# RMS norm with ReLU on one core: hardware loops with explicit semaphores, stores moved to Pool's software queue

## The chip, the cores and the metric

The kernel runs on one core of one Trainium2 chip; the other cores are idle. The metric is the device time of one execution in microseconds (us), as a median of several runs. The profiled execution has a "span", which is about 2 us shorter than the device time. All runs quoted here were with a granted clock of 1.0.

The engines matter as follows. ScalarE (ACT in the profile) squares and sums the rows. VectorE (DVE) scales them. SyncE (SP) only issues transfers and waits. Pool (GpSimd) does almost nothing in the kernel before (four fills, 0.2 us). Sixteen DMA engines move all data between HBM and the on-chip memory (SBUF): the page counts 33.56 MB read from HBM and 33.55 MB written.

## The reference

```python
x = randn(16, 1024, 512)            # float32; gamma = ones(512), eps = 1e-5
rms = np.sqrt(np.mean(x ** 2, axis=-1, keepdims=True) + eps)
out = np.maximum(x / rms * gamma, 0)
```

The input has 33.55 MB and the output as many. Each byte is read once and written once, so at least 67.11 MB must move.

## The kernel before

The 16,384 rows are cut into 8 chunks of 128 partitions x 16 rows x 512 numbers, 4.19 MB each. A chunk is loaded by one transfer, computed in place in two groups of 8 rows per partition, and stored by one transfer. There are six chunk buffers ("slots"), so the last two loads wait for the first two stores.

```python
def load(i):  nc.sync.dma_start(out=slot[i % nslots], in_=xv[i])
def store(i): nc.sync.dma_start(out=ov[i], in_=slot[i % nslots])

def compute(i):
    xt = slot[i % nslots]
    for g in range(ngroups):                       # 2 groups of 8 rows
        a, b = g * G, (g + 1) * G
        for j in range(a, b):
            nc.scalar.activation(out=junk, in_=xt[:, j, :], func=ACTF.Square,
                                 accum_out=ss[i][:, j:j + 1])
        nc.scalar.activation(out=rms[i][:, a:b], in_=ss[i][:, a:b],
                             func=ACTF.Sqrt, bias=eps_sb, scale=inv_d)
        nc.vector.tensor_mul(out=xt[:, a:b, :], in0=xt[:, a:b, :], in1=gammaG())
        nc.vector.reciprocal(out=rstd[i][:, a:b], in_=rms[i][:, a:b])
        for j in range(a, b):
            nc.vector.tensor_scalar(out=xt[:, j, :], in0=xt[:, j, :],
                scalar1=rstd[i][:, j:j + 1], scalar2=0.0,
                op0=ALU.mult, op1=ALU.max)
# ... (gamma is broadcast to all partitions; 6 loads are issued, 6 chunks computed)
nxt = nslots
for i in range(nchunks):
    store(i)
    if i >= 1 and nxt < nchunks:
        load(nxt); compute(nxt); nxt += 1
```

Everything is unrolled, and a framework places the waits. All loads and stores stand in one line on SyncE's hardware queue.

## Time and profile before

| | |
|---|---|
| time, median | 164.2 us (164.16 to 164.38, 3 runs) |
| span | 162.0 us |
| bytes moved | 67.11 MB |
| one 32 KB packet on one engine | 1.213 us, 27.0 GB/s |
| the engines' shortest total | 2,048 packets / 16 x 1.213 us = 155.3 us |
| first packet starts, last one ends | 1.75 us, 160.64 us |

First come lines of the profile's page: the span; the busy time of the engines; the busy share of VectorE and of the DMA engines in 40 equal slices (tenths); the queue with its packets, MB and share of the 16 engines' time; and the chain of waits by engine.

```profile
span 162.0 us, 554 instructions
...
DVE 124.6 (77%) x164; ACT 98.5 (61%) x274; POOL 0.2 (0%) x4
...
DVE  1001299999999999999999999999999999920000
...
DMA  6999899999999999998999999999999999999990
...
q1 hardware_dynamic: 2304, 67.11, 96.9%
...
DVE 74%; DMA 8%; ACT 3%; issue 2%; DVEq 0%
```

The DMA engines are busy from end to end (96.9%); VectorE is busy for 77% and has nothing to do in the last four slices. The chain of waits names VectorE first, with 74%. That chain follows only semaphores; it doesn't know that the last stores stand in line behind others. So the row of slices, not the chain, tells the bound here.

The rate is 433 GB/s, except for a dip to 385 where the first loads end and the stores begin (56 to 64 us).

Now VectorE. These are the groups of instructions of the page: count, total busy us and mean ns of one, then idle time before them.

```profile
L78 DVE TENSOR_TENSOR slot<-slot,gamma_sb 128x4096 f32<-128x4096 f32 x16 | 70.7, 4418 | 4.2 <-ACT junk L74 4.2
L81 DVE TENSOR_SCALAR slot<-slot,rstd 128x512 f32<-128x512 f32 x128 | 52.1, 481 | 0.6
```

And this is one group of 8 rows in time order (start us, length us, engine, line, operation), followed by the end of VectorE's work and the last store.

```profile
26.83 4.42 DVE L78 TENSOR_TENSOR slot<-slot,gamma_sb 128x4096 f32<-128x4096 f32 x1
31.17 0.19 DVE L79 RECIPROCAL rstd<-rms 128x8 f32<-128x8 f32 x1
31.40 3.26 DVE L81 TENSOR_SCALAR slot<-slot,rstd 128x512 f32<-128x512 f32 x8
34.57 4.42 DVE L78 TENSOR_TENSOR slot<-slot,gamma_sb 128x4096 f32<-128x4096 f32 x1
```

```profile
141.32 1.67 DVE L81 TENSOR_SCALAR slot<-slot,rstd 128x512 f32<-128x512 f32 x4
143.01 0.33 SPq L62 DMA_DIRECT2D out_dram<-slot  x1
```

One group takes 34.57 - 26.83 = 7.74 us: a product over 8 rows (4.33 to the next start), a reciprocal (0.23) and eight scalings (0.396 each). The last store is issued at 143.01 us, 19 us before the end. So VectorE has about 5 us to spare. This is an estimate: the first 15 of 16 chunk transfers take 15/16 x 155.3 = 146 us from 1.75 us on, and with the dip the engines would run dry near 149 us; the last store must be ready about 1 us before that.

### The profile page before, as it was taken

The numbers are of one execution on the slowest core, as the hardware profiler recorded it, in microseconds if no ns is written. First come the engines' busy times: TensorE is split into PE (matmuls) and PEld (weight loads), VectorE is DVE, ScalarE is ACT, GpSimd is POOL, SyncE is SP. The second block draws the span as 40 slices with busy tenths as digits, with TensorE's granted clock in tenths as the row PEclk, the third lists the DMA queues.
The fourth block names the chain that finished last, engine by engine and source line by source line (L and its number), as shares of the span: only waits on it lengthen the run. The fifth ranks groups of instructions, "written<-read, shape, count | busy, mean of one in ns | idle before, by whom it ended". The sixth has DMA issues, their size and how long they took to land.

```text
span 162.0 us, 554 instructions
## 1 busy us (share of the span) xinstructions
DVE 124.6 (77%) x164; ACT 98.5 (61%) x274; POOL 0.2 (0%) x4
## 2 busy tenths in 40 slices
DVE  1001299999999999999999999999999999920000
ACT  2107999999999999999999199901998000000000
POOL 0000000000000000000000000000000000000000
DMA  6999899999999999998999999999999999999990
GB/s 227 421 405 502 388 413 493 390 421 477 396 421 471 396 388 388 461 445 388 463 437 404 453 445 404 453 437 396 461 429 445 429 421 445 429 421 445 437 413 16
DMA packets 2315, 67.14 MB, mean 414 GB/s; under 512 B 260, under 2 KB 260, under 8 KB 264
## 3 DMA queue, kind: packets, MB, share of 16 engines
q1 hardware_dynamic: 2304, 67.11, 96.9%
q14 instruction: 3, 0.02, 0.0%
q10 hardware_dynamic: 8, 0.01, 0.0%
HBM read 33.56 MB, written 33.55 MB: 414 GB/s over the span
## 4 chain that ended last, share of the span: by engine, by line
DVE 74%; DMA 8%; ACT 3%; issue 2%; DVEq 0%
DVE slot L78 43%; DVE slot L81 30%; DMA slot<-in_x_dram 8%; ACT junk L74 3%; DVE rstd L79 1%; DVEq L133 0%
## 5 line engine op out<-in xcount | busy, mean ns | idle before, releaser
L74 ACT ACTIVATE junk<-slot 128x512 f32<-128x512 f32 x128 | 76.8, 600 | 23.0 <-DMA slot<-in_x_dram 19.5
L78 DVE TENSOR_TENSOR slot<-slot,gamma_sb 128x4096 f32<-128x4096 f32 x16 | 70.7, 4418 | 4.2 <-ACT junk L74 4.2
L81 DVE TENSOR_SCALAR slot<-slot,rstd 128x512 f32<-128x512 f32 x128 | 52.1, 481 | 0.6
L74 ACT ACTIVATION_READ_ACCUMULATOR junk<-slot 128x1 f32 x128 | 23.8, 186 | 0.0
L93 DVE LOAD_MASK_SELECT gamma_sb<-gseed x1 | 0.0, 14 | 12.8 <-DMA gseed<-in_gamma_dram 12.8
L76 ACT ACTIVATE rms<-ss,eps_sb 128x8 f32<-128x8 f32 x16 | 4.8, 301 | 0.5
L74 ACT ACT_TABLE_LOAD x1 | 1.3, 1283 | 3.2 <-issue 3.2
L79 DVE RECIPROCAL rstd<-rms 128x8 f32<-128x8 f32 x16 | 3.1, 194 | 0.0
L76 ACT ACT_TABLE_LOAD x1 | 1.3, 1283 | 0.0
L86 DVE MEMSET gseed<- 128x512 f32 x1 | 0.5, 485 | 0.9 <-PEq L119 0.9
L93 DVE STREAM_SHUFFLE gamma_sb<-gseed 128x512 f32<-128x512 f32 x1 | 0.7, 721 | 0.0
L119 POOL MEMSET const-bfloat16-1.0<- 128x1 bf16 x1 | 0.1, 101 | 0.0
L119 POOL MEMSET const-uint8-127<- 128x1 uint8 x1 | 0.1, 101 | 0.0
L119 POOL MEMSET const-float32-0.0<- 128x1 f32 x1 | 0.1, 99 | 0.2 <-issue 0.2
L119 POOL MEMSET const-float32-1.0<- 128x1 f32 x1 | 0.1, 98 | 0.0
L87 DVE MEMSET eps_sb<- 128x1 f32 x1 | 0.1, 59 | 0.0
## 6 DMA issues: line engine op xcount, KB each, us to landing
slot<-in_x_dram SPq DMA_DIRECT2D x8, 4096.0 KB, 30.6
out_dram<-slot SPq DMA_DIRECT2D x8, 4096.0 KB, 35.4
gseed<-in_gamma_dram ACTq DMA_DIRECT2D x4, 2.0 KB
```

The source lines that it names most:

```text
L74: nc.scalar.activation(out=junk, in_=xt[:, j, :], func=ACTF.Square, accum_out=ss[i][:, j:j + 1])
L76: nc.scalar.activation(out=rms[i][:, a:b], in_=ss[i][:, a:b], func=ACTF.Sqrt, bias=eps_sb, scale=inv_d)
L78: nc.vector.tensor_mul(out=xt[:, a:b, :], in0=xt[:, a:b, :], in1=gammaG())
L79: nc.vector.reciprocal(out=rstd[i][:, a:b], in_=rms[i][:, a:b])
L81: nc.vector.tensor_scalar(out=xt[:, j, :], in0=xt[:, j, :], scalar1=rstd[i][:, j:j + 1], scalar2=0.0, op0=ALU.mult, op1=ALU.max)
L86: nc.vector.memset(gseed, 0.0)
L87: nc.vector.memset(eps_sb, eps)
L93: nc.vector.stream_shuffle(gamma_sb, gseed, [0] * 32)
L119: nc = _bacc.Bacc("TRN2", target_bir_lowering=False, num_devices=1)
```

## The change

The change moves the stores from SyncE's queue to Pool's software queue (`software_dynamic` in the profile; Pool is busy for at least 0.53 us with each issue), and holds the first store until the fourth load has landed. ScalarE and VectorE each run a hardware loop of 16 turns with addresses taken from registers, and all waits become explicit semaphores. TensorE merely passes on "chunk has landed". VectorE's arithmetic is regrouped: the multiplications by the row's factor and by gamma become one fused instruction per row, and the max becomes one large instruction per group. The square root's table is loaded ahead of time (the trace of before has two table loads of 1.28 us). ScalarE's scratch output gets room for eight rows instead of one; its squares then come 0.61 us apart instead of 0.75.

```diff
-    def store(i): nc.sync.dma_start(out=ov[i], in_=slot[i % nslots])
+    def store(i): nc.gpsimd.dma_start(out=ov[i], in_=slot_ap(i)).then_inc(sem_st[i], 16)
+    # SyncE
+    for i in range(nchunks):
+        if i >= nslots:
+            nc.sync.wait_ge(sem_st[i - nslots], 16)
+        load(i)
+    # Pool
+    nc.gpsimd.wait_ge(sem_ld[3], 16)                 # the fourth load
+    for i in range(nchunks):
+        nc.gpsimd.wait_ge(done, per * (i + 1))       # per = 2 groups in a chunk
+        store(i)
     # ScalarE: ... the same squares and square roots, in Fori(0, 16), Sqrt table preloaded
-            nc.vector.tensor_mul(out=xt[:, a:b, :], in0=xt[:, a:b, :], in1=gammaG())
-            nc.vector.reciprocal(out=rstd[i][:, a:b], in_=rms[i][:, a:b])
-            for j in range(a, b):
-                nc.vector.tensor_scalar(out=xt[:, j, :], in0=xt[:, j, :],
-                    scalar1=rstd[i][:, j:j + 1], scalar2=0.0, op0=ALU.mult, op1=ALU.max)
+        with nc.vector.Fori(0, ngroups) as gi:
+            nc.vector.wait_ge(sq, 1); nc.vector.sem_inc(sq, -1)
+            base = nc.vector.snap((gi % (nslots * per)) * (G * d))
+            col = nc.vector.snap(gi * G)
+            nc.vector.reciprocal(out=rstd[:, bass.ds(col, G)],
+                                 in_=rms[:, bass.ds(col, G)]).then_inc(sv, 1)
+            nc.vector.wait_ge(sv, 1); nc.vector.sem_inc(sv, -1)
+            for j in range(G):
+                row = slots[:, bass.ds(base + j * d, d)]
+                r = nc.vector.scalar_tensor_tensor(out=row, in0=row,
+                    scalar=rstd[:, bass.ds(col + j, 1)], in1=gamma_sb,
+                    op0=ALU.mult, op1=ALU.mult)
+                if j == G - 1: r.then_inc(sv, 1)
+            nc.vector.wait_ge(sv, 1); nc.vector.sem_inc(sv, -1)
+            nc.vector.tensor_scalar_max(out=blk, in0=blk, scalar1=0.0).then_inc(done, 1)
```

More of the change, by code (lines that the diff above doesn't have):

```diff
@@ L31 @@
     inv_d = 1.0 / d
-    xv = x2.rearrange("(c p k) d -> c p k d", p=P, k=16)
-    ov = out2.rearrange("(c p k) d -> c p k d", p=P, k=16)
     K = 16
@@ L38 @@
     nslots = 6
-    ngroups = K // G
+    ngroups = rows // G
+    per = K // G
+    xv = x2.rearrange("(c p k) d -> c p k d", p=P, k=K)
+    ov = out2.rearrange("(c p k) d -> c p k d", p=P, k=K)
     singles = ctx.enter_context(tc.tile_pool(name="singles", bufs=1))
-    slots = ctx.enter_context(tc.tile_pool(name="slots", bufs=1))
-    small = ctx.enter_context(tc.tile_pool(name="small", bufs=1))
     psum = ctx.enter_context(
         tc.tile_pool(name="psum", bufs=1, space=bass.MemoryType.PSUM))
-    ctx.enter_context(tc.manual_schedule())
     gseed = singles.tile([P, d], F32, name="gseed")
@@ L51 @@
     eps_sb = singles.tile([P, 1], F32, name="eps_sb")
-    junk = psum.tile([P, d], F32, name="junk")
-    slot = [slots.tile([P, K, d], F32, name=f"slot{s}") for s in range(nslots)]
-    ss = [small.tile([P, K], F32, name=f"ss{i}") for i in range(nchunks)]
-    rms = [small.tile([P, K], F32, name=f"rms{i}") for i in range(nchunks)]
-    rstd = [small.tile([P, K], F32, name=f"rstd{i}") for i in range(nchunks)]
+    ss = singles.tile([P, rows], F32, name="ss")
+    rms = singles.tile([P, rows], F32, name="rms")
@@ new lines @@
+    rstd = singles.tile([P, rows], F32, name="rstd")
+    slots = singles.tile([P, nslots * K * d], F32, name="slots")
+    junk = psum.tile([P, G, d], F32, name="junk")
+    sem_ld = [tc.alloc_semaphore(f"ld{i}") for i in range(nchunks)]
+    sem_st = [tc.alloc_semaphore(f"st{i}") for i in range(nchunks)]
+    sem_g = tc.alloc_semaphore("gam")
+    sem_e = tc.alloc_semaphore("epsr")
+    sem_z = tc.alloc_semaphore("zero")
+    ready = tc.alloc_semaphore("ready")
+    sq = tc.alloc_semaphore("sq")
@@ L58, in load, with slot_ap @@
+    done = tc.alloc_semaphore("done")
+    sa = tc.alloc_semaphore("sa")
+    sv = tc.alloc_semaphore("sv")
+    def slot_ap(i):
+        s = (i % nslots) * K * d
+        return slots[:, s:s + K * d].rearrange("p (k d) -> p k d", d=d)
     def load(i):
-        nc.sync.dma_start(out=slot[i % nslots], in_=xv[i])
+        nc.sync.dma_start(out=slot_ap(i), in_=xv[i]).then_inc(sem_ld[i], 16)
     def store(i):
-        nc.sync.dma_start(out=ov[i], in_=slot[i % nslots])
-    def gammaG():
-        g = gamma_sb[:]
-        return bass.AP(tensor=g.tensor, offset=g.offset,
-                       ap=[g.ap[0], [0, G], g.ap[1]])
@@ L69, in compute @@
-    def compute(i):
-        xt = slot[i % nslots]
-        for g in range(ngroups):
-            a, b = g * G, (g + 1) * G
-            for j in range(a, b):
-                nc.scalar.activation(out=junk, in_=xt[:, j, :], func=ACTF.Square,
-                                     accum_out=ss[i][:, j:j + 1])
-            nc.scalar.activation(out=rms[i][:, a:b], in_=ss[i][:, a:b],
-                                 func=ACTF.Sqrt, bias=eps_sb, scale=inv_d)
-            nc.vector.tensor_mul(out=xt[:, a:b, :], in0=xt[:, a:b, :], in1=gammaG())
-            nc.vector.reciprocal(out=rstd[i][:, a:b], in_=rms[i][:, a:b])
-            for j in range(a, b):
-                nc.vector.tensor_scalar(
-                    out=xt[:, j, :], in0=xt[:, j, :],
-                    scalar1=rstd[i][:, j:j + 1], scalar2=0.0,
-                    op0=ALU.mult, op1=ALU.max)
@@ L86 @@
-    nc.vector.memset(gseed, 0.0)
-    nc.vector.memset(eps_sb, eps)
-    for q in range(0, P, 32):
-        nc.scalar.dma_start(out=gseed[q:q + 1, :], in_=gamma[None, :])
-    for i in range(min(nslots, nchunks)):
-        load(i)
-    nc.vector.stream_shuffle(gamma_sb, gseed, [0] * 32)
-    for i in range(min(nslots, nchunks)):
-        compute(i)
-    nxt = nslots
-    for i in range(nchunks):
-        store(i)
-        if i >= 1 and nxt < nchunks:
-            load(nxt)
-            compute(nxt)
-            nxt += 1
+        nc.gpsimd.dma_start(out=ov[i], in_=slot_ap(i)).then_inc(sem_st[i], 16)
@@ new lines @@
+    ctx.enter_context(tc.manual_schedule(engines={mybir.EngineType.SP}))
+    with tc.tile_critical():
+        for i in range(nchunks):
[3 more added lines that the diff above has]
+        for i in range(nchunks):
+            nc.tensor.wait_ge(sem_ld[i], 16)
+            nc.tensor.sem_inc(ready, per)
+        nc.gpsimd.wait_ge(sem_ld[min(3, nchunks - 1)], 16)
+        for i in range(nchunks):
+            nc.gpsimd.wait_ge(done, per * (i + 1))
+            store(i)
+        nc.vector.memset(gseed, 0.0).then_inc(sem_z, 1)
+        nc.vector.memset(eps_sb, eps).then_inc(sem_e, 1)
+        nc.scalar.wait_ge(sem_z, 1)
+        for q in range(0, P, 32):
+            nc.scalar.dma_start(out=gseed[q:q + 1, :],
+                                in_=gamma[None, :]).then_inc(sem_g, 16)
+        nc.scalar.preload_act_table(ACTF.Sqrt)
+        nc.scalar.wait_ge(sem_e, 1)
+        with nc.scalar.Fori(0, ngroups) as gi:
+            nc.scalar.wait_ge(ready, 1)
+            nc.scalar.sem_inc(ready, -1)
+            base = nc.scalar.snap((gi % (nslots * per)) * (G * d))
+            col = nc.scalar.snap(gi * G)
+            for j in range(G):
+                a = nc.scalar.activation(
+                    out=junk[:, j, :], in_=slots[:, bass.ds(base + j * d, d)],
+                    func=ACTF.Square, accum_out=ss[:, bass.ds(col + j, 1)])
+                if j == G - 1:
+                    a.then_inc(sa, 1)
+            nc.scalar.wait_ge(sa, 1)
+            nc.scalar.sem_inc(sa, -1)
+            nc.scalar.activation(out=rms[:, bass.ds(col, G)], in_=ss[:, bass.ds(col, G)],
+                                 func=ACTF.Sqrt, bias=eps_sb, scale=inv_d).then_inc(sq, 1)
+        nc.vector.wait_ge(sem_g, 64)
+        nc.vector.stream_shuffle(gamma_sb, gseed, [0] * 32)
+        with nc.vector.Fori(0, ngroups) as gi:
+            nc.vector.wait_ge(sq, 1)
+            nc.vector.sem_inc(sq, -1)
+            base = nc.vector.snap((gi % (nslots * per)) * (G * d))
+            col = nc.vector.snap(gi * G)
+            blk = slots[:, bass.ds(base, G * d)]
+            nc.vector.reciprocal(out=rstd[:, bass.ds(col, G)],
+                                 in_=rms[:, bass.ds(col, G)]).then_inc(sv, 1)
+            nc.vector.wait_ge(sv, 1)
+            nc.vector.sem_inc(sv, -1)
+            for j in range(G):
+                row = slots[:, bass.ds(base + j * d, d)]
+                r = nc.vector.scalar_tensor_tensor(
+                    out=row, in0=row, scalar=rstd[:, bass.ds(col + j, 1)], in1=gamma_sb,
+                    op0=ALU.mult, op1=ALU.mult)
+                if j == G - 1:
+                    r.then_inc(sv, 1)
+            nc.vector.wait_ge(sv, 1)
+            nc.vector.sem_inc(sv, -1)
+            nc.vector.tensor_scalar_max(out=blk, in0=blk, scalar1=0.0).then_inc(done, 1)
@@ L106 @@
+    with nc.sync.register("landed") as landed:
+        nc.sync.reg_mov(landed, 16)
+        for i in range(nchunks):
+            nc.sync.wait_ge(sem_st[i], landed)
 _INS = ['x', 'gamma', 'eps']
```

## The prediction

> **What bounds it now.** The transfers. The queue table has one queue with 67.11 MB, busy 96.9% of the 162.0 us span. Of the packets in the trace, 2,048 carry 32 KB and take 1.213 us each, on 16 engines: 128 x 1.213 = 155.3 us that no order of transfers shortens. The first starts at 1.75 us, the last ends at 160.6, its landing is seen near 162. From 4 us to 156 us the engines are full at about 433 GB/s, except a dip to 390 around 56 to 64 us (some 0.7 us lost). [...] So reordering can win about 3.5 us (2%), if start, tail and dip all vanished.
> The chain of waits names VectorE (74%), but VectorE ends at 143 us, 19 us before the end.
>
> **What the change does.**
> 1. Stores move to Pool's software queue and start only when load 3 has landed (estimate: 41 us; store 0 is ready near 35 us anyway). Loads 4 and 5 then share the engines with stores. Bytes are equal and a backlog exists throughout, so the engines should stay full[...].
> 2. VectorE work per group of 8 rows changes. Before, start to start: product 4.33, reciprocal 0.23, 8 scalings at 0.396 = 7.74 us. After: [...] Reciprocal and its wait 0.25[...]. Sum about 8.05 us, against 7.74: 16 x 0.3 = 5 us more. The loop's branch hides under the max.
> 3. ScalarE saves one table load (1.28), but VectorE must now wait for the first square root: first start near 19.9 instead of 19.1.
>
> VectorE then ends near 149 us (143 before). The last store needs the software issue (estimate 1 to 1.5 us), 9.7 us for 4.19 MB at 433 GB/s, and 1.4 to landing: 161 to 162. The engines' own floor is the same 159 to 162. Both limits meet; hardly anything shows.
>
> **Prediction: 164.9 us, range 162.4 to 170.0.** Faster by over 2%: 0.03; within: 0.72; slower: 0.25.
>
> **What would show it.** Bytes unchanged; two queues sharing about 97%, rate near 430 GB/s while both run. VectorE's fused multiply about 0.75 us long, the max about 2.28 us, groups 8.05 us apart; VectorE's end near 149 us; a small hole (1 to 3 us) in the transfers before the last store.
>
> **What would make it wrong.** A group over 8.3 us (exposed register steps[...]) makes VectorE the bound, at 16 us per us. [...] Software packets smaller or slower than 1.213 us per 32 KB would cost per cent for per cent. A faster result needs packets quicker than 1.21 us when reads and writes mix.

The traces, that of the changed kernel included, allow this estimate of a fused multiply: an eighth of the product (4.33 / 8 = 0.54 us), and what a scaling (0.396) takes beyond an eighth of the later max (2.20 / 8 = 0.275), 0.12, together 0.66 us; 0.663 was measured.

The sum of the span: 149 + 1 to 1.5 + 9.7 + 1.4 gives 161 to 162 us. But the number 164.9 held an allowance for loads and stores mixed on two queues. The first clause of item 1 has its estimate of 41 us from four loads of 9.7 us, from 1.75 us on; Pool's first issue, which that load released, started at 42.83 us. The software issue took 1.40 us (VectorE's end to the first packet). The loop's branch does hide: it takes 56 ns (median), and the first one starts at 25.8 us, while the max runs from 25.70 to 27.99. And VectorE sets the end of the transfers already at a group of 8.24 us, not only over 8.3.

## More of the kernel before

The next fence has the busy time of each engine in stretches of the span, with DMA share and GB/s in the last two columns.

```profile
core 0: us, DVE busy (x) ACT busy (x) POOL busy (x), PEclk, DMA share, GB/s
...
56.00:64.00 8.00, 7.96 (x12) 7.65 (x24) 0.00 (x0) 1.00 0.98 385
64.00:145.00 81.00, 78.63 (x105) 48.26 (x137) 0.00 (x0) 1.00 1.00 433
145.00:149.00 4.00, 0.00 (x0) 0.00 (x0) 0.00 (x0) 1.00 1.01 434
149.00:153.00 4.00, 0.00 (x0) 0.00 (x0) 0.00 (x0) 1.00 0.99 426
```

## The result

The changed kernel takes 166.81 us (median of 4 runs, 166.62 to 166.96); the kernel before took 164.29 us (4 runs). The ratio is 1.0151, with a 95% interval of 1.0132 to 1.0169: slower by 1.5%. Ratios here are the mean time of one kernel's fast runs over that of the other's of the same rounds, so not quite the ratio of the medians quoted.

These are the lines of the changed kernel's page that answer to those of before, with Pool's slices and the second queue added.

```profile
span 165.1 us, 1010 instructions
...
DVE 126.0 (76%) x164; ACT 86.3 (52%) x273; POOL 5.7 (3%) x12
...
DVE  1001198989898989898989898989898989896000
...
POOL 0000000000401000100010001000100010001000
DMA  5999999999989999999999999999999999990982
...
q1 hardware_dynamic: 1152, 33.55, 47.9%
q0 software_dynamic: 1152, 33.55, 47.1%
```

The slices have a new feature: the DMA row ends in 9, 0, 9, 8, 2. In one slice, a fortieth of the span, no packet starts. The stretches show it closely (columns as before; a packet counts where it starts):

```profile
64.00:145.00 81.00, 76.53 (x99) 38.71 (x124) 2.67 (x5) 1.00 1.01 434
145.00:149.00 4.00, 4.00 (x7) 0.00 (x0) 0.00 (x0) 1.00 0.91 393
149.00:153.00 4.00, 2.47 (x2) 0.00 (x0) 0.53 (x1) 1.00 0.00 0
153.00:159.00 6.00, 0.00 (x0) 0.00 (x0) 0.00 (x0) 1.00 1.02 437
```

From 149 to 153 us no packet starts, while VectorE works for 2.47 us and Pool for 0.53. By the packet records the engines run dry one after another up to 149.74 us, and the first packet of the last store starts at 153.01. The rate from 64 to 145 us, where loads and stores run side by side on two queues, is 434 GB/s; before it was 433. So neither loads and stores mixed nor the software queue slowed the stream.

The groups of VectorE and the first turn of its loop in time order:

```profile
L131 DVE SCALAR_TENSOR_TENSOR slots<-slots,rstd,gamma_sb 128x512 f32 x128 | 86.2, 747 | 4.8 <-DVEq L128 4.8
L138 DVE TENSOR_SCALAR slots<-slots x16 | 36.7, 2294 | 2.4 <-DVEq L137 0.2
...
L125 DVE RECIPROCAL rstd<-rms x16 | 3.2, 197 | 4.3 <-DVEq L121 4.3
```

```profile
19.65 0.20 DVE L125 RECIPROCAL rstd<-rms  x1 [4.31 <-DVEq L121]
20.15 5.39 DVE L131 SCALAR_TENSOR_TENSOR slots<-slots,rstd,gamma_sb 128x512 f32 x8 [0.30 <-DVEq L128]
25.70 2.29 DVE L138 TENSOR_SCALAR slots<-slots  x1 [0.16 <-DVEq L137]
27.90 0.20 DVE L125 RECIPROCAL rstd<-rms  x1
```

One turn takes 27.90 - 19.65 = 8.25 us instead of 7.74. The reciprocal's length is 0.20 us, yet the first multiply starts 0.50 us after it; the bracket puts 0.30 us of that down to VectorE's own sequencer, at the wait of L128. The sequencer has a register step before every multiply (the columns are the shortest, median and longest duration in ns):

```profile
L131 DVEq FUSED_REGOPS  x128: 93/93/115, 20.0 to 144.8; - x128
```

For the later multiplies these steps don't show: they start 0.663 us apart, although each lasts 0.747, and all of VectorE's 4.8 us of idle time at this line is at the 16 waits of L128, 0.30 us each. So only the wait, the decrement and the first step are exposed. Before the max another 0.16 us is.

The end of the kernel:

```profile
143.78 5.39 DVE L131 SCALAR_TENSOR_TENSOR slots<-slots,rstd,gamma_sb 128x512 f32 x8 [0.30 <-DVEq L128]
149.32 2.29 DVE L138 TENSOR_SCALAR slots<-slots  x1
151.91 0.53 POOL L74 DMA_DIRECT2D out_dram<-slots  x1 [15.95 <-DVE slots L138]
```

VectorE ends at 151.61 us. The last store is issued at 151.91, its first packet starts at 153.01, its last ends at 162.92, and the span ends at 165.1.

From the packet records of both traces the difference of the spans can be added up. "Engine idle" below is the sum over the 16 engines, divided by 16.

| term, us | before | after | difference |
|---|---|---|---|
| first packet starts | 1.75 | 1.96 | +0.20 |
| engines idle from 145 to 156 us (the hole) | 0.00 | 4.00 | +4.00 |
| engines idle after 156 us, up to the last packet's end (uneven ends) | 2.02 | 0.09 | -1.93 |
| last packet's end to end of span | 1.39 | 2.18 | +0.79 |
| all else (packets' own time, small gaps) | 156.87 | 156.87 | 0.00 |
| span | 162.03 | 165.10 | +3.06 |

The changed kernel has a hole of 4 us, but it also lacks a loss that the kernel before has: there, one DMA engine ends at 160.64 us while the median engine ends at 158.5. After the hole all engines start the last store together and end together.

### The profile page after: what moved, and what is told of

Same layout as the page of the kernel before. It is cut to its first block, busy times and chain, and to the rows that moved or that the text cites. A ratio compares the mean times of both kernels' runs of the same rounds, so it can differ in the third digit from the quotient of the medians.

```text
span 165.1 us, 1010 instructions
## 1 busy us (share of the span) xinstructions
DVE 126.0 (76%) x164; ACT 86.3 (52%) x273; POOL 5.7 (3%) x12
## 5 line engine op out<-in xcount | busy, mean ns | idle before, releaser
L107 ACT ACTIVATE junk<-slots 128x512 f32 x128 | 74.5, 582 | 34.9 <-ACTq L103 34.6
L131 DVE SCALAR_TENSOR_TENSOR slots<-slots,rstd,gamma_sb 128x512 f32 x128 | 86.2, 747 | 4.8 <-DVEq L128 4.8
L138 DVE TENSOR_SCALAR slots<-slots x16 | 36.7, 2294 | 2.4 <-DVEq L137 0.2
L107 ACT ACTIVATION_READ_ACCUMULATOR junk<-slots x128 | 24.0, 187 | 0.0
L74 POOL DMA_DIRECT2D out_dram<-slots x8 | 5.5, 687 | 146.5 <-DVE slots L138 104.1
L125 DVE RECIPROCAL rstd<-rms x16 | 3.2, 197 | 4.3 <-DVEq L121 4.3
L114 ACT ACTIVATE rms<-ss,eps_sb x16 | 4.8, 301 | 3.0 <-ACTq L113 3.0
```

The source lines that it names most:

```text
L74: nc.gpsimd.dma_start(out=ov[i], in_=slot_ap(i)).then_inc(sem_st[i], 16)
L107: a = nc.scalar.activation(out=junk[:, j, :], in_=slots[:, bass.ds(base + j * d, d)], func=ACTF.Square, accum_out=ss[:, bass.ds(col + j, 1)])
L114: nc.scalar.activation(out=rms[:, bass.ds(col, G)], in_=ss[:, bass.ds(col, G)], func=ACTF.Sqrt, bias=eps_sb, scale=inv_d).then_inc(sq, 1)
L125: nc.vector.reciprocal(out=rstd[:, bass.ds(col, G)], in_=rms[:, bass.ds(col, G)]).then_inc(sv, 1)
L131: r = nc.vector.scalar_tensor_tensor(out=row, in0=row, scalar=rstd[:, bass.ds(col + j, 1)], in1=gamma_sb, op0=ALU.mult, op1=ALU.mult)
L138: nc.vector.tensor_scalar_max(out=blk, in0=blk, scalar1=0.0).then_inc(done, 1)
```

## The experiments

The theory was that VectorE's longer turn lets the engines run dry before the last store, and that this hole is the loss. The main rivals were that the software queue, or loads and stores mixed, make the transfers slower throughout, or that holding back the first store costs time. Ten kernels were run, all correct.

### 1. The last store in two halves

```diff
-        for i in range(nchunks):
+        for i in range(nchunks - 1):
             nc.gpsimd.wait_ge(done, per * (i + 1))
             store(i)
+        last = nchunks - 1
+        for h in range(per):                 # half a chunk: its 8 rows per partition
+            nc.gpsimd.wait_ge(done, per * last + h + 1)
+            nc.gpsimd.dma_start(out=ov[last][:, h*G:(h+1)*G, :],
+                in_=slot_ap(last)[:, h*G:(h+1)*G, :]).then_inc(sem_st[last] if h == 0 else sem_half, 16)
```

> The changed kernel with one edit: the last store goes out in two halves, each when its group of 8 rows is done. Theory (VectorE ends at 151.6 us, so the last store leaves a hole of about 4.3 us in the transfers, and that hole is the whole loss): the first half is ready at 143.3 us and fills the hole, the second needs 4.9 us instead of 9.7; span about 160.5 to 161, time about 162.5 us, below both kernels. Rival (software descriptors, or mixing reads and writes, make the transfers slower throughout): bytes, queue and mixing are the same, so time stays at 166 to 167 us.

It took 163.70 us (163.47 to 163.83), ratio 0.9962 (0.9946 to 0.9979). Stretches and the two issues in the trace:

```profile
145.00:149.00 4.00, 4.00 (x7) 0.00 (x0) 0.00 (x0) 1.00 0.97 418
149.00:153.00 4.00, 2.39 (x2) 0.00 (x0) 0.53 (x1) 1.00 1.00 430
```

```profile
143.59 0.53 POOL L95 DMA_DIRECT2D out_dram<-slots  x1 [7.71 <-DVE slots L145]
...
149.25 2.29 DVE L145 TENSOR_SCALAR slots<-slots  x1
151.84 0.53 POOL L95 DMA_DIRECT2D out_dram<-slots  x1 [7.71 <-DVE slots L145]
```

VectorE ends as late as before the edit (151.54 us), but the stretch from 149 to 153 us now moves 430 GB/s. Filling the hole wins 3.1 us and brings the changed kernel below the kernel before. The result is 1.2 us higher than expected: the engines end unevenly again (0.59 us idle after 156 us), the last packet ends at 159.31, and from there to the end it is 2.4 us, where I had reckoned with 1.4. The rival is refuted, as the queue, the mixing and the bytes are the same.

### 2. VectorE's old arithmetic in the loop

```diff
-            (reciprocal; 8 x scalar_tensor_tensor; wait; one tensor_scalar_max)
+            nc.vector.reciprocal(out=rstd[:, bass.ds(col, G)], in_=rms[:, bass.ds(col, G)])
+            # blk3, gG: the 8 rows, and gamma repeated 8 times; gamma's broadcast before the loop also gets a wait
+            nc.vector.tensor_mul(out=blk3, in0=blk3, in1=gG).then_inc(sv, 1)
+            nc.vector.wait_ge(sv, 1); nc.vector.sem_inc(sv, -1)
+            for j in range(G):  # ... tensor_scalar(row, rstd, 0.0, mult, max); the last signals done
```

> The changed kernel with VectorE's old arithmetic inside its loop (one product of 4096 elements, then 8 scalings with the max), all else as changed. Theory: a group then lasts 0.13 + 4.42 + 0.3 + 8 x 0.396 = 8.0 us instead of 8.24, VectorE ends near 148 us, the hole shrinks from 4.3 to under 1 us; time about 163.2 us. Rival (transfers slower throughout): 166 to 167 us.

It took 163.47 us (163.27 to 163.59), ratio 0.9948 (0.9932 to 0.9965). I expected a turn of 8.0 us and 163.2 us. A turn lasts 7.82 us, VectorE ends at 144.66 us, and the engines never idle between 145 and 156 us. Loops, software queue and the late first store are all still there, so none of them is the loss by itself.

### 3. The changed kernel without hardware loops

```diff
-        with nc.vector.Fori(0, ngroups) as gi:         # and the same for nc.scalar
-            base = nc.vector.snap((gi % (nslots * per)) * (G * d))
-            col = nc.vector.snap(gi * G)
+        for gi in range(ngroups):
+            base = (gi % (nslots * per)) * (G * d)
+            col = gi * G
```

> The changed kernel with both loops unrolled: same operations, same semaphores, but fixed addresses. Theory: the 0.30 us between reciprocal and first multiply falls to under 0.1 and the 0.16 before the max to about 0.05; a group lasts about 7.9 us, VectorE ends near 146 us, no hole; time 162.5 to 163.5 us. If the instruction fetches of the kernel before are what made one of its 16 engines end 1.2 us after the rest, they come back here with such a late engine. Rival (transfers slower throughout): 166 to 167 us. If the exposed steps are not due to the register addresses, a group stays at 8.2 and the time too.

It took 164.04 us (163.93 to 164.15), ratio 0.9983 (0.9966 to 1.0000). I expected 162.5 to 163.5; the turn got shorter by half of what I thought. The last turn in the trace:

```profile
140.49 0.20 DVE L125 RECIPROCAL rstd<-rms 128x8 f32<-128x8 f32 x1
140.83 5.39 DVE L131 SCALAR_TENSOR_TENSOR slots<-slots,rstd,gamma_sb 128x512 f32<-128x512 f32 x8
146.37 2.29 DVE L138 TENSOR_SCALAR slots<-slots 128x4096 f32<-128x4096 f32 x1
```

The reciprocal is followed by the first multiply after 0.34 us (0.50 in the loop), and the step before the max is unchanged. So the loop with its register addresses costs 0.15 us per turn; run 10 gives the share of the explicit waits. The turn is 8.09 us and VectorE ends at 148.66, 2.95 us earlier than in the changed kernel (16 turns of 0.15 us, and a start 0.56 us earlier); a hole of 1.13 us remains, where I expected none; the span is 162.14, also 2.95 us shorter. One for one is what a kernel bound by VectorE's end must show.

The question of the fetches (packets of kind `instruction` in the trace: three in the kernel before, none in the changed kernel) got no answer here: four came back, but after the hole all engines start the last store together and end within 0.15 us. One number in this expectation and in that of run 7 is misread: in the kernel before, the late engine ends 1.69 us after the next (160.64 against 158.95), not 1.2. The packet that ends at 159.43 is the late engine's own last but one.

### 4. Stores on SyncE's hardware queue

```diff
-        nc.gpsimd.dma_start(out=ov[i], in_=slot_ap(i)).then_inc(sem_st[i], 16)
+        nc.sync.dma_start(out=ov[i], in_=slot_ap(i)).then_inc(sem_st[i], 16)
+        # SyncE: 6 loads; then store 0, store 1, load 6, store 2, load 7, stores 3 to 7, each after its wait
+        # Pool's waits go, that for the fourth load too
```

> The changed kernel with the stores on SyncE's hardware queue, in the order of the kernel before; loops and VectorE as changed. Theory: VectorE still ends near 151.6 us and a hole of 4 us remains; only the issue of the last store gets shorter (0.3 to 0.8 us); time 166.0 to 166.6 us. Rival (the software queue or the mixing is the loss): about 164 us or less, since both are gone.

It took 165.48 us (165.34 to 165.64), ratio 1.0072 (1.0055 to 1.0088). Of the 4 us of idle, 3.05 remain without any software queue:

```profile
149.00:152.00 3.00, 2.29 (x1) 0.00 (x0) 0.00 (x0) 1.00 0.00 0
```

I expected 166.0 to 166.6 us and a hole of 4. The edit wins 1.3 us in time and 1.56 in the span, which is about the sum of three terms. VectorE ends 0.30 us earlier, as it started earlier. From VectorE's end to the first packet it is 151.32 to 152.17 = 0.85 us, with Pool 151.61 to 153.01 = 1.40 us. From the last packet's end to the end of the span it is 1.45 us, with Pool 2.18. So Pool's queue costs about 1.3 us of the 1.56, and the start the rest.

### 5. No waiting for the fourth load

```diff
-        nc.gpsimd.wait_ge(sem_ld[min(3, nchunks - 1)], 16)
```

> The changed kernel without the wait for the fourth load before the first store. Theory (the end is set by when VectorE finishes the last rows): VectorE runs as before, the first store starts at 36.5 instead of 42.8 us, the hole before the last store stays at 4 us; time 166.8 us, within 0.3. Rival (holding the stores back costs time): 1 to 3 us less. Second rival (holding them back helps, mixing hurts): more than 167.2 us.

It took 166.73 us (166.66 to 166.78), ratio 1.0147 (1.0127 to 1.0167), with a hole of 3.99 us. The first store starts 6.5 us sooner and nothing follows from it. This part of the change is neutral.

This run showed something else. The first fence is the changed kernel around its first store, the second this run (columns: start us, length us):

```profile
42.18 2.30 DVE L138 TENSOR_SCALAR slots<-slots  x1
...
42.83 1.77 POOL L74 DMA_DIRECT2D out_dram<-slots  x1 [42.38 <-DMA slots<-in_x_dram]
...
53.03 0.53 POOL L74 DMA_DIRECT2D out_dram<-slots  x1 [8.43 <-DVE slots L138]
```

```profile
36.34 0.67 POOL L74 DMA_DIRECT2D out_dram<-slots  x1 [35.90 <-DVE slots L137]
```

The third is from run 6, where the first issue falls into a product (34.57 to 38.99 us):

```profile
34.96 0.67 POOL L62 DMA_DIRECT2D out_dram<-slot  x1 [34.52 <-DVE slot L81]
```

Where the first issue falls into VectorE's large max (42.18 to 44.48 us), Pool needs 1.77 us for it and ends 0.12 us after the max. Run 1 shows the same: 1.67 us, ending 0.12 us after its max (42.10 to 44.40). Where no max runs, it needs 0.67, beside a product too. It cost nothing here, as the transfers had a backlog: this run, without it, is as fast (166.73 against 166.81 us). All later stores are issued just after a max, since they wait for it, and take 0.53 us.

### 6. The kernel before with its stores on Pool's queue

```diff
-        nc.sync.dma_start(out=ov[i], in_=slot[i % nslots])
+        nc.gpsimd.dma_start(out=ov[i], in_=slot[i % nslots])
```

> The kernel before with one edit: its stores go out on Pool's software queue. Theory: still bound by the transfers, VectorE still ends at 143 us, no hole; the last packet ends near 160.6 us and the software queue adds only the 0.8 us that the changed kernel shows between last packet and end (2.2 against 1.4): about 165.0 us. Rival (software descriptors or mixing slow the packets): 166 us or more.

It took 163.22 us (162.96 to 163.92), ratio 0.994 (0.9918 to 0.9962). My expectation of 165.0 missed: this line of the change, taken alone, wins 1.1 us. No engine is late by more than 0.4 us (VectorE ends later than before, at 146.4 us, as the last load lands later and VectorE waits 3.3 us for its rows; that costs nothing). The last packet ends at 159.35 us instead of 160.64, although each packet still takes 1.21 us.

### 7. Halved last store, unrolled

The edit is that of run 3 on top of run 1.

> The run with the last store in halves, with both loops unrolled. No hole in either. If the instruction fetches of unrolled code delay one of the 16 engines (the kernel before has three, and one engine that ends 1.2 us after the next and 1.9 after the median), then four fetches come back here, one engine ends about 1 to 2 us after the rest, and the time is 164.4 to 165 us, although VectorE ends about 3 us earlier than in the loop version (163.7 us). If fetches don't matter: 163.4 to 163.8 us, engines ending within 1 us.

It took 164.17 us (163.98 to 164.22), ratio 0.9988 (0.9972 to 1.0004). The last engine ends at 160.12 us, 0.76 us after the next (159.36), and four instruction fetches appear among the packets. That lies between my two expectations. It is 0.5 us worse than the loop version, though VectorE ends 2.9 us sooner. The intervals of the two ratios just overlap, and they come from different calls, so the fetches are a likely part of the uneven ends, not a settled one.

### 8. Stores on ScalarE's hardware queue

If a second queue helps, it needn't be Pool's. The kernel before got its stores on ScalarE's queue, each placed behind the squares of two later chunks, so that ScalarE doesn't stop for long.

```diff
-        nc.sync.dma_start(out=ov[i], in_=slot[i % nslots])
+        nc.scalar.dma_start(out=ov[i], in_=slot[i % nslots])
...
+    lag = 2
+    for i in range(nchunks + lag):
+        if i < nchunks:
+            if i >= nslots: load(i)
+            compute(i)
+        if i >= lag: store(i - lag)
```

> The kernel before with its stores on ScalarE's hardware queue (each store two chunks behind the squares). It asks why the kernel before ran 1.1 us faster with its stores on Pool's software queue. If a second queue of any kind is the reason (loads and stores no longer in one line, so no engine falls behind): last packet near 159.3 us, time about 162.8 to 163.2 us. If the software queue as such is the reason: one late engine near 160.6 us and 164.3 us.

It took 162.68 us (162.37 to 162.84), ratio 0.9895 (0.9878 to 0.9912), slightly better than expected for "a second queue of any kind", and the best of all. From its page:

```profile
span 161.0 us, 520 instructions
...
DMA  7999999999999999999999999999999999999993
...
q1 hardware_dynamic: 1152, 33.55, 49.2%
q10 hardware_dynamic: 1160, 33.56, 48.4%
```

The two queues share the bytes evenly (q10 carries the stores and the 8 packets of gamma), and the last packet ends at 159.47 us. The short end of a hardware queue stays: 1.53 us from the last packet to the end, against 1.73 in run 6.

### 9. Loops, old arithmetic, hardware queue

The edits of runs 2 and 4 together, meant to have no hole, no fetches and no software queue.

> A version meant to beat both: the loops of the change, VectorE's old arithmetic, stores on SyncE's hardware queue in the old order. Theory: VectorE ends near 144.5 us, no hole; no instruction fetches, so no late engine, last packet near 159.2 us; 1.4 us from there to the end (hardware queue): span about 160.6, time 162.4 to 162.8 us. Rival (the loops win nothing, the software queue is what helped the two good runs): 164.2 us as before.

It took 163.29 us (162.84 to 163.52), ratio 0.9938 (0.9919 to 0.9957): better than both kernels, but 0.5 us short of what I expected. It differs from run 2 in the queue of the stores alone, with the order and the waits that go with it, and the two are as fast (163.29 and 163.47 us, intervals overlapping): in the loop version a second queue wins nothing. Its last packet ends 0.6 us sooner (159.17 against 159.77), and Pool's longer way to the end (2.30 against 1.57) takes that back. There are no fetches within the body, yet one engine still ends 0.7 us after the next (159.77 against 159.08). So fetches alone don't make the late engine; with one queue it comes back in part.

### 10. The change's arithmetic in the kernel before

The loop over groups of the kernel before got the reciprocal, the eight fused multiplies and the large max; nothing else was touched.

> The kernel before with the change's VectorE arithmetic alone (fused multiply by row, one big max), still unrolled and with stores on SyncE's queue. Theory: a group lasts 7.95 us (0.23 + 0.07 + 7 x 0.663 + 0.75 + 0.04 + 2.21), VectorE starts near 20.7 and ends near 148 us, just before the transfers run out of work at 149 us: no hole or one under 0.7 us, time 164.3 to 164.9 us. If the arithmetic alone caused the loss, it would be 166 us or more here too.

It took 164.02 us (162.65 to 164.36), ratio 0.9967 (0.9936 to 0.9997), just below the 164.3 to 164.9 expected; its executions spread more than those of any other run. A group takes 7.87 us (the expectation's step of 0.07 us doesn't show: its other terms alone add up to 7.87), VectorE ends at 146.75 us, before the transfers run dry, and no hole appears. The arithmetic alone costs 0.13 us per group (7.87 against 7.74), which fits into the slack. The explicit waits add 0.22 (8.09 in run 3) and the register addresses 0.15 (8.24). Arithmetic and waits together already leave the hole of 1.13 us of run 3; all three leave 4.00.

### The runs side by side

All but the last column are from the traces (us), the last is the median time. Run 7 has its numbers above.

| run | group on VectorE | VectorE ends | engines idle 145 to 156 | last packet ends | next-to-last engine's end | time |
|---|---|---|---|---|---|---|
| before | 7.74 | 142.98 | 0.00 | 160.64 | 158.95 | 164.29 |
| after | 8.24 | 151.61 | 4.00 | 162.92 | 162.90 | 166.81 |
| 1 last store halved | 8.24 | 151.54 | 0.00 | 159.31 | 159.12 | 163.70 |
| 2 old arithmetic | 7.82 | 144.66 | 0.00 | 159.17 | 158.94 | 163.47 |
| 3 unrolled | 8.09 | 148.66 | 1.13 | 159.97 | 159.94 | 164.04 |
| 4 SyncE queue | 8.24 | 151.32 | 3.05 | 162.09 | 162.05 | 165.48 |
| 5 early stores | 8.24 | 151.42 | 3.99 | 162.71 | 162.69 | 166.73 |
| 6 before, Pool queue | 7.74 | 146.39 | 0.00 | 159.35 | 158.99 | 163.22 |
| 10 before, new arithmetic | 7.87 | 146.75 | 0.00 | 160.66 | 160.24 | 164.02 |
| 8 before, ScalarE queue | 7.74 | 143.06 | 0.00 | 159.47 | 159.23 | 162.68 |
| 9 loops, SyncE, old arithmetic | 7.82 | 144.63 | 0.00 | 159.77 | 159.08 | 163.29 |

## Why the prediction was right, and where it was off

The measured 166.81 us lies inside the range of 162.4 to 170.0, and the class (within 2%) was right. So was the mechanism in the main, but the nearness of the number is in part luck.

- *164.9 us.* The prediction's own chain ends at a span of 161 to 162, which is a time of 163 to 164. So 164.9 seems to hold about 1 us for mixing, an allowance that no trace showed. That loss didn't come, while the turn and the end of the span cost more: the number was 1.9 us too low, the chain of the span 3 to 4.
- *The transfers bound the kernel before, with about 3.5 us to win at most.* Nothing contradicts it; the best of ten variants won 1.6 us.
- *VectorE's turn gets longer and spends its slack.* Right, but mis-sized: 8.05 us was predicted, 8.24 measured. The arithmetic held: a fused multiply of about 0.75 us and a max of 2.28 were predicted, 0.747 and 2.294 measured. Too small was what stands around it: reciprocal, waits and register steps measured 0.50 + 0.16 = 0.66 us, against 0.25 for "reciprocal and its wait" and the allowance for the steps. The turn is 0.19 us longer than predicted, or 3.0 us in sixteen turns. VectorE started 0.25 us earlier than predicted (19.65 against 19.9), so it ended about 2.6 us later (151.6 against 149).
- *A hole of 1 to 3 us before the last store.* It came, with 4.0 us, for the same reason. Runs 1 and 2 show that it is the loss, and run 3 that the span follows VectorE's end one for one.
- *Software issue 1 to 1.5 us.* Right: 1.40 us from VectorE's end to the first packet. *1.4 us to landing* was too low: the end of the span came 2.18 us after the last packet. With hardware queues it was 1.39 to 1.57.
- *A loss by loads and stores mixed and by the software queue* (the allowance of item 1). The sign was wrong. The packets didn't slow down (434 GB/s), and in the unrolled kernel before a second queue won 1.1 us (run 6) or 1.6 us (run 8, whose order of stores also differs); in the traces the last packet ends 1.2 to 1.3 us sooner, as no engine lags. In the loop version it won nothing (runs 2 and 9). I had seen the late engine in the trace of before and taken it for granted.
- *Pool held up by VectorE's max*. It showed once in the changed kernel, for 1.1 us (1.77 against 0.67), off the critical path. It neither stretched VectorE (the 16 maxes take 2.294 to 2.296 us) nor starved the queue.

So the change is a sum of gains and losses: a second queue helps where one engine lags and fewer fetches may, while a longer turn, one undivided last store and Pool's later end cost more. What stays open is why one queue lets an engine fall behind. Instruction fetches are a part at most (runs 7 and 9), and these comparisons rest on one trace each. The kept traces cut both ways. An engine's packets follow one another within nanoseconds (in the kernel before, a packet starts within 5 ns of the end of each of the three fetches), so its chain can be followed back: the two late engines of run 10 (160.24 and 160.66 us) are those that took its three fetches. But in the kernel before the engine with two of the three ends near 158.9 us, and runs 6 and 8 have three fetches in mid-stream, like the kernel before, and no late engine.

## What to carry to other kernels

In a kernel bound by transfers, ask when the last producer must be finished for the last transfer to start without a hole, and count that slack before making a per-turn cost longer: here 0.5 us per turn, 16 turns and 5 us of slack decided it. Make the last transfer small, so that a late producer delays few bytes. Try loads and stores on a queue each even when one queue already keeps the engines full (433 GB/s here, 434 with two queues; it won 1.1 and 1.6 us in the unrolled kernel, nothing in the loops), and look at how evenly the 16 engines end, which the average share of busy time doesn't show.

## Other figures of this case

- From 64 to 145 us the rate was 433 GB/s before, 434 in the changed kernel and 429 in run 8, so a second queue didn't raise it. But stores on a queue of their own won 0.6% (Pool) and 1.05% (ScalarE), as the last of the 16 engines ended at 159.4 us instead of 160.6. In the loop version the separate queue won nothing (runs 2 and 9).
- The fused multiply by row, 128x512 in float32, took 0.747 us, 0.663 us from start to start, while the scaling by a row factor took 0.396 from start to start.
- In VectorE's loop the register step took 93 ns (median) and was exposed only after a wait: 0.15 us per turn, plus about 0.1 us for a separate wait and decrement after the reciprocal (0.34 us unrolled, against 0.23 with the framework's wait).
- From the last packet to the end of the span it was 1.7 to 2.4 us with Pool's queue, against 1.4 to 1.6 with hardware queues only.
- In the kernel before, three fetches of 309 to 325 ns stood among the data packets, and the packet that followed each took 1.33 to 1.87 us instead of 1.21. How much of the time this costs stays open (run 7 hints at up to 0.5 us; runs 6 and 8 have three such fetches and no late engine).
